# Slot beginnings between the last features, reciprocals spread by TensorE, output weights in the last slots, and RWKV factors without GpSimd

## The chip, the cores and the metric

The kernel runs on one core of one Trainium2 chip. The metric is the device time of one execution in microseconds, here as the median of a few runs. The engines of the core are named as the profile names them: PE is TensorE (matmuls; PEld its weight loads), DVE is VectorE, ACT is ScalarE, POOL is GpSimd, and SP is SyncE, which issues all DMAs of this kernel in one queue.

## What is computed

One inference step of a two-layer backbone for 1024 latent tokens and 128 prompt tokens, width 1024. Each layer projects the modulated input into three head groups, combines them in one output projection and adds it to the residual stream. The three parts that the change touches:

```python
def rwkv_step(S, inp):
    r_t, w_t, k_t, v_t, kk_t, a_t = inp
    sa = jnp.einsum('ebhvk,ebhk->ebhv', S, -kk_t)
    S = (S * w_t[..., None, :] + sa[..., :, None] * (kk_t * a_t)[..., None, :]
         + v_t[..., :, None] * k_t[..., None, :])
    return S, jnp.einsum('ebhvk,ebhk->ebhv', S, r_t)
...
    def one_block(args):
        qn_b, qr_b = args
        s = (jnp.einsum('bqhd,bkhd->bhqk', qn_b, kn)
             + jnp.einsum('bqhr,bkr->bhqk', qr_b, kr)).astype(jnp.float32) * SOFTMAX_SCALE
        p = jax.nn.softmax(s, axis=-1).astype(v.dtype)
        return jnp.einsum('bhqk,bkhd->bqhd', p, v)
...
    out = jnp.concatenate([y_rw, y_mla, y_lru], axis=-1) @ P['w_out'][l]
    x = layer_norm(ALPHA * x + gate * out, P['ln_g'][l], P['ln_b'][l])
```

The RWKV scan (4 heads, 2 directions) is done in chunks of 64 tokens: with cumulated decays every token's key, receptance and removal vectors become factors, and a chunk is a few small matmuls and a triangular inverse.

## The kernel before

Prompt and latent tokens stand in one array of 1152 columns, 9 tiles of 128 tokens, 18 chunks of 64. Operands of the large products are split in two parts (`mm3`: high x high, high x low, low x high). Each of the two layers goes through these stages.

*Token projections and queries*, then *features*: `order` lists 16 blocks of 128 columns of the input projection; for each, `feature(n_, j)` computes three blocks of 384 tokens, 24 matmuls each, into a PSUM tile `ps_a`, of which there are three. From the tenth feature on `RW_AT` starts `rwkv_tile(i)` for the 9 tiles: the **factor stage**. `rwkv_tile` loads the tile (`rw`), the key norms (`nkk`, in the single buffer `mxb`), computes log decays `lw_` and their cumulated sums `Lc` (two scans), and for each direction `d` the four factors: `z` and `r` in `abz` (`zr`), `k` and `b` in `ls` (`bk`), written to DRAM. Three of the products are made by GpSimd (lines 585, 593, 594). Between the features also stand pieces of the adaLN projection (`adaln_piece`), whose row `ep` is copied from PSUM by DVE before TensorE may use it.

*Beginnings*: nine value products `value(i)` and a tenth for the prompt, the prompt's two attention units (`ups`), and everything that the slot plan puts into slots -6 to -1: keys, loads and splits of queries, first row maxima (`max_q`, into the single PSUM tile `ps_b`), the first windows of the RWKV scan and their inverse. All of it stands in one block at a raised priority (line 1247), so a scheduler may put it ahead of work that was written before it.

*Slots*: 16 attention units (8 heads, two halves of 512 latent tokens) of three slots each, 48 slots a layer. A slot has fixed blocks A0, three score products, G, A1, B, values, C, sums, S; `at(slot, block, f, ...)` puts pieces of the RWKV windows, the adaLN rest, the next units' row maxima and group norms into them. In the slots the order of PE, DVE and ACT is the order of the code (`in_line`); DMAs and GpSimd are placed by the scheduler. At its last slot a unit's row sums are in PSUM; `sums` copies them, sends them through DRAM (`l_d`) to 128 x 4, `finish` takes the reciprocal there, sends it through DRAM again to 128 x 256 (`lr`), and `gate` multiplies.

*Output projection*: the 16 blocks of the output weights are loaded (`kp`), split into `wo_h` and `wo_l`, the gate rows are loaded and their bias added by GpSimd, the first weights of the next layer are loaded and split, and then nine output tiles follow, in `ORDER` (8, 2, 3, 4, 5, 6, 1, 0, 7), each 48 matmuls of 512 columns.

## Time and profile before

| what | value |
|---|---|
| median of three runs | 2005.73 us (2003.27 to 2010.9) |
| the profiled execution | 2003.78 us, span of its instructions 2001.9 us |
| busy share of the span | PE 91%, PEld 76%, DVE 60%, ACT 46%, POOL 34% |
| mean granted TensorE clock | 0.944 of full speed |
| layer 0: factors, beginnings, slots, hand-over | 336 to 448, to 512, to 889 (43 slots) and 940 us |
| layer 1: the same | 1340 to 1440, to 1491, to 1863 (43 slots) and 1890 us |

The granted clock of 1.00 is 2.4 GHz, half of it 1.2 GHz; a mean between them says for how much of a stretch the lower level held. A busy matmul side is not a matmul side at its peak. The rows below come from one profiled execution; windows are microseconds from the start of its span. In the rows DVE, ACT and PE stand with line 116 and 121, those of the helpers that record every instruction, so groups are told apart by their tiles.

### The profile page before, as it was taken

Reading aid. Unit: us, or ns where it says so; the run is one execution under the profiler, and the core shown is the slowest. Engines: PE = TensorE matmul, PEld = TensorE weight load, DVE = VectorE, ACT = ScalarE, POOL = GpSimd, SP = SyncE. Lnnn points to the kernel's source line nnn. Section 1 sums busy time; section 2 is a strip of 40 time slices with the busy share of each in tenths; the row PEclk is TensorE's granted clock in tenths of the full one; section 3 lists DMA queues with packets and bytes.
Section 4 is the critical chain, followed back from the end, with each engine's and each line's share of the span. In section 5 each row is a group of like instructions: output and inputs, shape, how many; then the busy total and the mean of one; then the engine's idle time right before and its main releaser. Section 6 shows DMA issues by size and latency. Waiting matters only on the chain.

```text
span 2001.9 us, 47694 instructions
## 1 busy us (share of the span) xinstructions
PE 1815.0 (91%) x18494; PEld 1527.9 (76%) x18494; DVE 1202.3 (60%) x2472; ACT 924.4 (46%) x2069; POOL 684.7 (34%) x1159
## 2 busy tenths in 40 slices
PE   6899998888899999994998999997779999998898
PEld 4798887786687787763877999997657778776686
DVE  6744445883456565764778443569735565666476
ACT  2533566442454554553235426675325455555421
POOL 1410011461434434322545100126424444441353
PEclk8999999887899999997998999998869999999999
DMA  8334444653335444437443252435533443334542
GB/s 298 109 96 153 131 122 139 208 179 107 90 95 126 115 114 103 118 107 221 151 138 111 93 173 87 121 113 173 172 84 66 108 93 99 89 89 141 154 155 85
DMA packets 346242, 256.34 MB, mean 128 GB/s; under 512 B 116968, under 2 KB 285600, under 8 KB 344992
## 3 DMA queue, kind: packets, MB, share of 16 engines
q1 hardware_dynamic: 346016, 253.30, 43.3%
q8 instruction: 145, 2.38, 0.5%
q14 instruction: 81, 0.66, 0.1%
HBM read 174.38 MB, written 78.78 MB: 126 GB/s over the span
## 4 chain that ended last, share of the span: by engine, by line
PE 68%; DVE 12%; DMA 10%; ACT 3%; issue 3%; SPq 2%; POOL 1%; DVEq 0%; ACTq 0%; POOLq 0%
PE ps_a L121 46%; PE ps_pv L121 7%; PE ps_b L121 5%; PE ps_rw L121 4%; PE ps_cx L121 4%; DVE ls L116 4%; DVE rw L116 3%; DVE sm L116 2%; DVE t L116 1%; DMA mxb<-inv_d 1%; DMA kp<-in_wout_dram 1%; DMA t<-zr_d 1%; DMA ls<-l_d 1%; DMA l_d<-sm 1%; ACT t L116 1%
## 5 line engine op out<-in xcount | busy, mean ns | idle before, releaser
L121 PE MATMUL ps_a<-t,t 128*128 128x384 f32 (+3 forms) x6048 | 708.8, 296 | 20.7 <-DVE t L116 5.4
L121 PEld LDWEIGHTS ps_a<-t,t 128*128 128x128 f32 (+1 forms) x6048 | 650.9, 167 | 48.5 <-ACT pe L116 14.1
L116 DVE TENSOR_REDUCE sm<-ps_b 128x1 f32<-128x1024 f32 (+1 forms) x164 | 181.3, 1106 | 123.4 <-PE ps_b L121 122.1
L121 PE MATMUL ps_a<-q,t 128*128 128x512 f32 (+1 forms) x912 | 233.6, 402 | 8.9 <-DVE ep L116 4.0
L116 ACT ACTIVATE pe<-ps_a 128x512 f32<-128x512 f32 (+1 forms) x296 | 168.3, 575 | 137.1 <-PE ps_a L121 125.3
L121 PEld LDWEIGHTS ps_a<-q,t 128*128 128x128 f32 x912 | 172.7, 198 | 54.1 <-issue 11.5
L121 PE MATMUL ps_a<-t,q 128*128 128x512 f32 (+1 forms) x544 | 161.6, 381 | 0.0
L116 DVE TENSOR_TENSOR t<-kp,t 128x512 fp32r<-128x512 f32 (+2 forms) x128 | 86.5, 704 | 87.9 <-ACT t L116 87.6
L121 PE MATMUL ps_a<-t,kp 128*128 128x512 f32 (+1 forms) x304 | 118.0, 390 | 22.7 <-DVE kp L116 22.7
L121 PE MATMUL ps_b<-t,q 96*128 96x512 f32 (+1 forms) x400 | 116.2, 388 | 22.9 <-DVE sm L116 17.0
L116 ACT CAST t<-kp 128x512 fp32r<-128x512 f32 (+2 forms) x128 | 73.3, 601 | 119.8 <-DMA kp<-in_wft_dram 47.7
L121 PE MATMUL ps_pv<-pe,t 128*64 128x256 f32 x928 | 125.3, 391 | 0.0
L121 PEld LDWEIGHTS ps_a<-t,q 128*128 128x128 f32 x544 | 100.0, 188 | 21.9
L520 POOL TENSOR_TENSOR rw<-rw 128x512 f32<-128x512 f32 (+1 forms) x24 | 20.0, 832 | 263.8 <-ACT rw L116 172.8
L121 PEld LDWEIGHTS ps_b<-t,q 96*128 96x128 f32 x400 | 67.5, 201 | 50.0 <-DVE sm L116 23.3
L855 POOL TENSOR_TENSOR t<-t 64x15 f32<-64x15 f32 (+2 forms) x270 | 72.4, 268 | 76.9 <-DVE t L116 43.0
L116 DVE TENSOR_TENSOR t<-ps_a,t 128x512 f32<-128x512 f32 (+2 forms) x106 | 65.5, 625 | 40.3 <-ACT t L116 33.5
L157 POOL TENSOR_TENSOR sm<-sm,nhalf 128x1 f32<-128x1 f32 (+1 forms) x54 | 34.3, 637 | 155.5 <-DVE sm L116 150.1
L121 PEld LDWEIGHTS ps_pv<-pe,t 128*64 128x64 f32 x928 | 59.8, 137 | 34.2 <-issue 8.6
L121 PEld LDWEIGHTS ps_a<-t,kp 128*128 128x128 f32 x304 | 58.3, 192 | 35.4 <-DVE kp L116 23.5
L1066 POOL TENSOR_TENSOR q<-q,q 96x512 fp32r<-96x512 f32 x36 | 47.3, 1314 | 100.6 <-ACT q L116 99.2
L121 PEld LDWEIGHTS ps_cx<-t,t 128*64 128x64 f32 (+1 forms) x1752 | 65.5, 138 | 20.3 <-ACT t L116 8.9
(258 smaller groups left out, 3253.7 us busy)
## 6 DMA issues: line engine op xcount, KB each, us to landing
kp<-in_wft_dram SPq DMA_DIRECT2D x64, 256.0 KB
kp<-in_wmod_dram SPq DMA_DIRECT2D x64, 256.0 KB
rw<-in_x_dram SPq DMA_DIRECT2D x36, 256.0 KB
gate_d<-pe SPq DMA_DIRECT2D x48, 192.0 KB
bk_d<-ls SPq DMA_DIRECT2D x36, 256.0 KB
zr_d<-abz SPq DMA_DIRECT2D x36, 256.0 KB
t<-bk_d SPq DMA_DIRECT2D x18, 512.0 KB
t<-zr_d SPq DMA_DIRECT2D x36, 256.0 KB
```

The lines of the kernel that those rows point to most:

```text
L116: return lambda *a, **k: in_line(getattr(self.eng, op)(*a, **k))
L121: return in_line(nc.tensor.matmul(*a, **k))
L157: gtt(out, t[:, :n], nhalf.to_broadcast([128, n]), op=POW)
L520: gtt(q_, a_, a_, op=MUL)
L855: gtt(tv, U_[0:64, 0:t, t:t + 1].to_broadcast([64, t, n]), X[0:64, t:t + 1, t:16].to_broadcast([64, t, n]), op=MUL)
L1066: gtt(qo[0:96], ql, qh[0:96], op=SUB)
```

## The change

`rwkv_tile`: the difference `Lc - lw_`, its exponential and GpSimd's three products go. The exponentials of `Lc` shifted by one token serve for `z`; the two products of each direction that are left are made by DVE, and the scale-and-add of `lw_` and of `k` and the copies into `wcs` by ScalarE. `finish`: the reciprocal is taken by DVE on the 128 x 128 sums in PSUM (`rl`), and four small matmuls with a constant (`two`) spread it over the output rows; no DRAM is passed; the factor 1/64 stands in the copy of the values (`u["o"]`). The gate's input is loaded earlier (`load_gate`), and GpSimd makes the last product. The beginnings are written out by hand between the parts of the last two features (`features` has become a generator), without the raised priority. The output weights are loaded and split in the last five slots, the gate rows get their bias in `adaln_piece`, the first output tiles are loaded before the last unit is finished, and the next layer's first weights come after two output tiles.

```diff
@@ rwkv_tile
-            vec_.tensor_scalar(fl(lw_), fl(tw), LWS, LWS, op0=MUL, op1=ADD)
+            act(fl(lw_), fl(tw), AF.Copy, bias=LWS, scale=LWS)
...
-                gtt(z, ch(Lc[:, d]), ch(lw_[:, d]), op=SUB)
-                act(z, z, AF.Exp)
                 act(r, ch(Lc[:, d]), AF.Exp)
                 act(b, ch(Lc[:, d]), AF.Exp, scale=-1.0)
                 if d == 0:
-                    vec_.tensor_copy(wcs[:, 0, q0:q0 + 2].rearrange("p q f -> p f q"), zr[:, :, :, 1, 63])
+                    sca_.copy(wcs[:, 0, q0:q0 + 2].rearrange("p q f -> p f q"), zr[:, :, :, 1, 63])
...
-                gtt(z, z, ch(nkk), op=MUL)
-                gtt(r, r, ch(r_), op=MUL)
+                at_, of_, end_ = (slice(1, 64), slice(0, 63), 0) if d == 0 else (slice(0, 63), slice(1, 64), 63)
+                sca_.copy(z[:, :, end_], ch(nkk)[:, :, end_])
+                vtt(z[:, :, at_], r[:, :, of_], ch(nkk)[:, :, at_], op=MUL)
+                vtt(r, r, ch(r_), op=MUL)
                 for f in range(2):
-                    vts(bk[:, f, :, 1], ta[:, d, f].rearrange("p (c t) -> p c t", c=2), kah[:, f:f + 1], omk[:, f:f + 1], op0=MUL, op1=ADD)
+                    act(bk[:, f, :, 1], ta[:, d, f].rearrange("p (c t) -> p c t", c=2), AF.Identity, bias=omk[:, f:f + 1], scale=kah[:, f:f + 1])
@@ sums, finish, gate
-                    ls = u["ls"] = W("ls", [128, 512])
-                    sca_.copy(ls[:, 0:128], u["sum"][:, 0:128])
-                    l_d = dram([4, 128], "l_d", 3)
-                    dma(l_d, ls[0:128:32, 0:128])
-                    u["lq"] = T("sm", [128, 16])
-                    dma(u["lq"][:, 0:4], l_d.rearrange("q (a c) -> (q a) c", c=4))
+                    u["rl"] = W("ls", [128, 128])
+                    vec_.reciprocal(u["rl"], u["sum"][:, 0:128])
...
+            ps = [P("a") for _ in range(2)]
+            for q_ in range(4):
+                r, c = (q_ // 2, q_ % 2) if u["q0"] < NS else (q_ % 2, q_ // 2)
+                R_ = slice(32 * q_, 32 * q_ + 32)
+                mm(ps[c][64 * r:64 * r + 64, 0:128], lhsT=two[R_], rhs=u["rl"][R_], start=True, stop=True)
+            for c in range(2):
+                vtt(u["o"][:, 128 * c:128 * c + 128], ps[c][:, 0:128], u["o"][:, 128 * c:128 * c + 128], op=MUL)
...
-            vtt(gm, gm, u["lr"], op=MUL)
+            gtt(gm, gm, u["o"], op=MUL)
@@ the plan of the slots
+        for x in range(2 * KT):
+            s_ = nslot - 5 + 5 * x // (2 * KT)
+            at(s_ - 1, "C", wo_load, x)
+            at(s_, "G", wo_split, x)
+        at(nslot - 1, "C", load_gates)
@@ the beginnings (cut)
+        more(2)
+        early(-6)
+        more(2)
+        early(-5)
...
+        early(-4)
+        value(0)
+        prompt_keys(0)
+        early(-3)
+        value(1)
+        max_last(ups[0])
+        value(2)
+        max_rows(ups[0])
+        early(-2)
...
@@ after the slots
+        load_out(0)
         finish(us[-1])
         gate(us[-1])
...
-        if l + 1 < layers:
-            w1 = first_weights(l + 1)
         for n_, i in enumerate(ORDER):
+            if n_ > 1:
+                load_out(n_)
+            if n_ == 2 and l + 1 < layers:
+                w1 = first_weights(l + 1)
```

How the change moves instructions is seen in three places. The first is VectorE in the factor stage of layer 0, one tile in its middle. `mxb` is the scaled key norm, `abz` holds z and r, `ls` holds k and b, `t<-kp` is a weight split and `pe` a gate feature. Before:

```order
L116 TENSOR_SCALAR ls_3589<-rw_617_3548,hv_278 128x2x64 x2
L116 SCALAR_TENSOR_TENSOR mxb_3539<-rw_613_3538,vec_111,mxb_3539 128x128 x2
L116 TENSOR_TENSOR ls_3572<-ls_3572 128x4x64
L116 TENSOR_TENSOR ls_3589<-ls_3589,rw_613_3538 128x4x64
L116 SCALAR_TENSOR_TENSOR rw_617_3548<-rw_617_3548,mxb_3539 128x256 x2
L116 TENSOR_TENSOR ls_3589<-ls_3589 128x4x64
L116 SCALAR_TENSOR_TENSOR ls_3572<-rw_617_3548,ls_3572 128x4x64
L116 SCALAR_TENSOR_TENSOR ls_3589<-rw_617_3548,ls_3589 128x4x64
```

VectorE at the same tile with the change:

```order
L116 SCALAR_TENSOR_TENSOR mxb_3541<-rw_613_3540,vec_111,mxb_3541 128x128 x2
L116 SCALAR_TENSOR_TENSOR rw_620_3569<-kc,rw_616_3549 128x256 x2
L116 TENSOR_TENSOR ls_3574<-ls_3574,rw_613_3540 128x4x64
L116 SCALAR_TENSOR_TENSOR rw_617_3550<-rw_617_3550,mxb_3541 128x256
L116 TENSOR_TENSOR t_4076<-kp_4089,t_4075 128x4x128
L116 TENSOR_TENSOR abz_3573<-abz_3573,mxb_3541 128x4x63
L116 TENSOR_TENSOR ls_3574<-ls_3574 128x4x64
L116 TENSOR_TENSOR ls_3590<-ls_3590,rw_613_3540 128x4x64
L116 SCALAR_TENSOR_TENSOR rw_617_3550<-rw_617_3550,mxb_3541 128x256
L116 SCALAR_TENSOR_TENSOR ls_3574<-rw_617_3550,ls_3574 128x4x64
L116 TENSOR_TENSOR abz_3589<-abz_3589,mxb_3541 128x4x63
```

The scale-and-add on `ls` has left VectorE's row, and the product of `abz` with the key norm, which GpSimd made, has come into it.

The second place is TensorE near the end of the features of layer 0. `ps_a<-t` are feature products, `kp,cS` and `kc,ep` an adaLN piece, `q,ckvh` value products, `ps_b` row maxima. Before, after the last feature:

```order
L121 MATMUL ps_a_4531<-kp_4527,cS 32x128 x4
L121 MATMUL ps_a_4531<-kp_4528,cS 32x128 x4
L121 MATMUL ps_a_4542<-kc,ep_4540 128x2
L121 MATMUL ps_a_4549<-q_4115,ckvh_326 128x512
L121 MATMUL ps_a_4549<-q_4116,ckvh_326 128x512
L121 MATMUL ps_a_4549<-q_4115,ckvl_327 128x512
L121 MATMUL ps_a_4554<-q_4115,ckvh_326 128x512
L121 MATMUL ps_a_4554<-q_4116,ckvh_326 128x512
```

TensorE with the change, three feature blocks before the last:

```order
L121 MATMUL ps_a_4436<-t_447,t_4076 128x384
L121 MATMUL ps_b_4612<-t_4113,q_4346 128x512 x2
L121 MATMUL ps_a_4469<-kp_4465,cS 32x128 x4
L121 MATMUL ps_a_4469<-kp_4466,cS 32x128 x4
L121 MATMUL ps_b_4640<-t_4113,q_4346 128x512 x2
L121 MATMUL ps_a_4480<-kc,ep_4478 128x2
L121 MATMUL ps_a_4483<-t_335,t_4075 128x384
```

The first row maxima, which stood behind the ten value products and the prompt, now stand among the features.

The third place is ScalarE in the last slots of layer 0. `pe` and `mxb` are exponentials of scores, `t<-kp` are splits of output weights, `ep` a unit's output. Before:

```order
L116 ACTIVATE pe_11068<-ps_a_11064 128x512
L116 CAST t_11146<-kp_11183 128x512
L116 CAST t_11146<-kp_11187 128x512
L116 CAST t_11146<-kp_11191 128x512
L116 COPY ep_11091<-ps_pv_10955 128x256
L116 CAST t_11146<-kp_11195 128x512
L116 COPY ls_11114<-ps_rw_10971 128x128
L116 CAST t_11147<-kp_11199 128x512
L116 CAST rw_1755_11258<-rw_1754_11256 128x512
```

ScalarE with the change, four slots before the last:

```order
L116 ACTIVATE pe_10867<-ps_a_10863 128x512
L116 ACTIVATE pe_10873<-ps_a_10869 128x512
L116 ACTIVATE mxb_10879<-ps_a_10875 128x512
L116 CAST t_10742<-kp_10840 128x512
L116 CAST t_10742<-kp_10842 128x512
L116 CAST t_10743<-kp_10844 128x512
L116 ACTIVATE ep_10921<-ps_pv_10727 128x256
L116 ACTIVATE pe_10947<-ps_a_10943 128x512
```

The splits that stood behind the last exponentials now stand between the exponentials of earlier slots.

## Rows read from the trace of the kernel before

**Rows 1.** Windows: start:end, length, busy us per engine (instructions), PE clock, DMA, GB/s.

```profile
336.00:448.00 112.00, 90.46 (x582) 84.53 (x581) 98.71 (x217) 54.59 (x160) 61.20 (x74) 0.88 0.56 184
448.00:512.00 64.00, 48.40 (x346) 37.99 (x346) 21.04 (x35) 15.88 (x39) 13.80 (x34) 0.72 0.41 119
512.00:889.00 377.00, 368.86 (x6158) 290.99 (x6157) 228.83 (x457) 192.72 (x433) 145.60 (x354) 1.00 0.43 107
889.00:940.00 51.00, 24.12 (x216) 14.50 (x214) 21.61 (x59) 21.67 (x45) 12.75 (x11) 0.77 0.67 205
1340.00:1440.00 100.00, 80.28 (x427) 74.19 (x426) 92.02 (x199) 47.91 (x148) 59.18 (x69) 0.86 0.46 156
1440.00:1491.00 51.00, 36.30 (x268) 26.90 (x268) 17.98 (x27) 13.78 (x35) 13.29 (x33) 0.67 0.49 135
1491.00:1863.00 372.00, 360.83 (x5891) 281.54 (x5890) 227.35 (x438) 196.62 (x443) 145.66 (x355) 0.99 0.39 97
1863.00:1890.40 27.40, 21.20 (x197) 13.27 (x197) 10.25 (x37) 13.28 (x30) 11.48 (x11) 0.98 0.49 144
```

**Rows 2.** Groups by form, 335 to 445: count | busy us, mean ns | idle before.

```profile
L116 DVE TENSOR_SCALAR ls<-rw,hv 128x128 f32<-128x128 f32 x35 | 16.8, 539 | 7.1 <-ACT rw L116 5.5 <-DMA bk_d<-ls 1.5
L116 DVE SCALAR_TENSOR_TENSOR rw<-rw,mxb 128x256 f32<-128x256 f32 x17 | 9.8, 603 | 0.0
L116 DVE SCALAR_TENSOR_TENSOR ls<-rw,ls 128x256 f32<-128x256 f32 x17 | 9.5, 578 | 0.1
L116 DVE TENSOR_TENSOR ls<-ls 128x256 f32<-128x256 f32 x17 | 9.2, 539 | 0.0
L116 DVE COPY wcs<-abz 128x4 f32<-128x4 f32 x18 | 7.1, 397 | 0.4 <-ACT abz L116 0.4
L116 DVE TENSOR_SCALAR rw<-rw 128x512 f32<-128x512 f32 x9 | 4.8, 539 | 0.2 <-ACT rw L116 0.2
...
L116 ACT ACTIVATE rw<-ps_rw,hv 128x128 f32<-128x128 f32 x36 | 10.5, 396 | 0.0
```

**Rows 3.** Timeline of layer 0's factors: start, us, engine, instruction.

```profile
343.60 0.84 POOL L594 TENSOR_TENSOR abz<-abz,rw 128x256 f32<-128x256 f32 x1 [0.24 <-DVE wcs L116]
343.77 0.96 DVE L116 TENSOR_TENSOR ls<-ls,rw 128x256 f32<-128x256 f32 x1
...
416.74 0.41 DVE L116 TENSOR_TENSOR ls<-ls,rw 128x256 f32<-128x256 f32 x1
```

**Rows 4.** Waits of PE, 336 to 448 and 448 to 512; chain of waits.

```profile
PE ps_a L121 <- DVE ep L116: 21.5, 5, 5.9
...
PE ps_b L121 <- DVE sm L116: 9.4, 6, 4.5
...
499.62 2.62 DMA ls<-l_d
```

**Rows 5.** Waits of PE from 889 to 941, and the chain of waits there.

```profile
PE ps_a L121 <- DVE kp L116: 21.5, 1, 21.5
...
929.98 7.07 DMA kp<-in_wtk_dram
```

**Rows 6.** Chain pieces in the slots of layer 0, and groups of VectorE by form.

```profile
862.06 1.45 PE ps_pv L121 x12
864.43 0.79 PE ps_rw L121 x24
...
L116 DVE RECIPROCAL sm<-sm 128x4 f32<-128x4 f32 x36 | 6.3, 174 | 20.6 <-DMA sm<-l_d 20.1
L116 DVE TENSOR_TENSOR_SCAN q<-rw,vec,q 128x512 f32<-128x512 f32 x8 | 10.3, 1283 | 0.2
L116 DVE TENSOR_REDUCE sm<-ps_b 128x1 f32<-128x1024 f32 x59 | 72.2, 1223 | 44.7 <-PE ps_b L121 43.9
```

**Rows 7.** Groups over the whole span: splits of weights on ScalarE and VectorE.

```profile
L116 ACT CAST t<-kp 128x512 fp32r<-128x512 f32 (+2 forms) x128 | 73.3, 601 | 119.8 <-DMA kp<-in_wft_dram 47.7 <-DMA kp<-in_wtk_dram 33.2 <-DMA kp<-in_wout_dram 28.3
L116 DVE TENSOR_TENSOR t<-kp,t 128x512 fp32r<-128x512 f32 (+2 forms) x128 | 86.5, 704 | 87.9 <-ACT t L116 87.6
```

More of the change, by code (lines that the diff above doesn't have):

```diff
@@ L689, in feature, with features @@
                 dma(gate_d[gi, :, bs], e)
-        for n_ in range(NFT):
-            if n_ == NFT - 2:
-                p_late = tc.cur_priority
+        def features(n_):
+            nonlocal ada_todo, wh, wl
             t = order[n_]
@@ L730, in hybrid_kernel @@
                 rwkv_tile(i)
+        for n_ in range(NFT - 2):
+            for _ in features(n_):
+                pass
         dma(lru_out[l], lru_fin)
@@ L746, in value @@
             (vec_.tensor_copy if i % 2 else sca_.copy)(val(i), ps)
-        for i in range(9):
-            value(i)
         lnx = sb.tile([128, 2, 2, 64], F32, name=f"lnx{l}", tag="lnx", bufs=1)
@@ L1123, in values @@
                     u["o"] = W("ep", [128, 256])
-                    sca_.copy(u["o"], u["pv"][:, 0:256])
+                    act(u["o"], u["pv"][:, 0:256], AF.Copy, scale=1 / 64)
         def sums(u):
@@ L1206, in hybrid_kernel @@
             at(s0 - 2, "S", max_rows, u)
-            if s0 + 5 < nslot:
-                at(s0 + 4, "G", finish, u)
-                at(s0 + 5, "G", gate, u)
-        for k_, todo_ in enumerate(ada_todo):
+            at(s0 + 2, "G", load_gate, u)
+            if s0 + 4 < nslot:
+                at(s0 + 3, "C", finish, u)
+                at(s0 + 4, "G", gate, u)
+        for k_, todo_ in enumerate(ada_todo[2:]):
             ada_ = adaln_piece(*todo_)
-            at(3 * k_ + 1, "S", next, ada_)
-            at(3 * k_ + 2, "A1", next, ada_, None)
-        ada_todo = []
+            at(5 * k_ // 2 + 1, "S", next, ada_)
+            at(5 * k_ // 2 + 2, "A1", next, ada_, None)
+        ada_todo = ada_todo[:2]
         CH = 7
@@ L1244, in hybrid_kernel @@
                     tail.append(gn)
-        with tc.high_priority(offset=tc.cur_priority - p_late):
-            value(9)
-            ups = [dict(h=4 * g, q0=NS, i=g, pe=[]) for g in range(2)]
-            for u in ups:
-                load_q(u)
-                split_q(u)
-            for g, u in enumerate(ups):
-                prompt_keys(g)
-                max_last(u)
-                max_rows(u)
-                scores(u, 0)
-                values(u)
-                sums(u)
-                finish(u)
-                gate(u)
-            for slot in range(min(s for s, _ in todo), 0):
-                for b in ("A0", "G", "A1", "B", "C", "S"):
-                    run(slot, b)
+        for x in range(2 * KT):
+            s_ = nslot - 5 + 5 * x // (2 * KT)
+            at(s_ - 1, "C", wo_load, x)
+            at(s_, "G", wo_split, x)
@@ new lines, in hybrid_kernel, with early, more, prompt @@
+        at(nslot - 1, "C", load_gates)
+        def early(slot):
+            for b in ("A0", "G", "A1", "B", "C", "S"):
+                run(slot, b)
+        assert min(s for s, _ in todo) == -6
+        last_features = (x for n_ in (NFT - 2, NFT - 1) for x in features(n_))
+        def more(n):
+            for _ in range(n):
+                next(last_features, None)
+        def prompt(u):
+            values(u)
+            sums(u)
+        ups = [dict(h=4 * g, q0=NS, i=g, pe=[]) for g in range(2)]
@@ new lines, in hybrid_kernel @@
+        for u, t_ in zip(ups, (promptq[:, 0:2], promptq[:, 2:4])):
+            u["qs"] = [t_[:, e] for e in range(2)]
+        more(2)
+        early(-6)
+        more(2)
+        early(-5)
+        more(1)
+        more(2)
+        for u in ups:
+            for t_ in u["qs"]:
+                nc.gpsimd.memset(t_[96:128].bitcast(F32), 0.0)
+            load_q(u)
+            split_q(u)
+            load_gate(u)
+        early(-4)
[3 more added lines that the diff above has]
+        value(1)
@@ new lines, in hybrid_kernel @@
+        max_last(ups[0])
+        value(2)
+        max_rows(ups[0])
+        early(-2)
+        value(9)
+        value(3)
+        scores(ups[0], 0)
+        prompt_keys(1)
+        value(4)
+        max_last(ups[1])
+        prompt(ups[0])
+        value(5)
+        early(-1)
+        max_rows(ups[1])
+        value(6)
+        scores(ups[1], 0)
+        value(7)
+        value(8)
+        finish(ups[0])
+        gate(ups[0])
+        prompt(ups[1])
+        todo.setdefault((0, "C"), []).insert(0, (finish, (ups[1],)))
@@ L1265, in hybrid_kernel @@
+        at(0, "S", gate, ups[1])
         line.update(on=True, last={})
@@ L1278, in hybrid_kernel, with load_out @@
         line["on"] = False
+        out_y = {}
+        def load_out(n_):
+            out_y[n_] = [W("pe" if n_ else "rw2", [128, 4, 128]) for _ in range(2)]
+            for j in range(2):
+                dma(out_y[n_][j], yT_d[ORDER[n_], :, 4 * j:4 * j + 4])
+        load_out(0)
         finish(us[-1])
```

75 lines of the change are left out of this document (37 added, 38 removed).

## The prediction

> **What bounds the kernel now.** First the page's engine shares, in the table above: TensorE's matmul side is busy 91% of the span, so a gain has to come from stretches where it is not busy or not at its upper clock. The stretches show where those are [rows 1]. The slots (512 to 889 and 1491 to 1863) have PE busy 368.86 of 377 and 360.83 of 372 us at a granted clock of 1.00 and 0.99, the upper level of 2.4 GHz: nothing to win there. Ahead of them in each layer lie two poorer stretches. While the RWKV factors are made (336 to 448, 1340 to 1440) PE is busy 90.46 of 112 us at clock 0.88 and 80.28 of 100 at 0.86, with DVE at 98.71 and 92.02 us: VectorE is the full engine, TensorE waits for it (21.5 us in five waits for the small `ep` copy alone, rows of which stand behind tile work in DVE's order [rows 4]) and falls to 1.2 GHz in between. Then come the beginnings of the slots (448 to 512, 1440 to 1491), where no engine is full, PE is busy 48.40 of 64 and 36.30 of 51 us and the clock is 0.72 and 0.67: a chain of single steps, one of them the reciprocals' trip through DRAM [rows 4]. After the slots of layer 0 (889 to 940) PE is busy 24.12 of 51 us; one wait of 21.5 us ends with DVE's split of the first output tile, which stood behind weight loads of the next layer [rows 5]. Layer 1 has less of that: 21.20 of 27.40 us.
>
> Counted at the upper clock, the work of TensorE is 90.46 x 0.88 + 48.40 x 0.72 = 114 us of the 176 from 336 to 512, and 80.28 x 0.86 + 36.30 x 0.67 = 93 of 151 in layer 1. So at most 62 + 58 us can be won ahead of the slots.
>
> **Factors without GpSimd.** A tile of 128 tokens is 2 directions; a layer has 9 tiles, 18 directions. DVE loses per layer 36 scale-and-add on 128 columns at 539 ns, 18 copies into `wcs` at 397 and 9 on 512 columns at 539: 19.4 + 7.1 + 4.9 = 31.4 us. It gains the two products that GpSimd did, 36 on 256 columns. While GpSimd works, such a DVE product takes 0.96 us, alone 0.41 [rows 3]; GpSimd's list is empty here afterwards, so I take 0.41: 14.8 us. The ends are 0.41 and 0.96 (34.6 us, which would eat the whole gain). The products that stay lose their slow share too: means of 603, 578 and 539 ns [rows 2] down to 415, 18 of each, 8.6 us. Net -25 us of DVE: 98.7 becomes 74 in layer 0, 92 becomes 67 in layer 1.
>
> ScalarE takes over: 36 on 128 columns at 396 ns (14.3 us), 9 on 512 columns at about the 601 of the weight casts [rows 7] (5.4), 36 tiny copies, not in the trace in this form; between 0.17 us, the smallest DVE row here [rows 6], and 0.40, I take 0.3 (10.8); it loses 18 exponentials, by the same row about 0.4 us each (7.2). Net +23: 54.6 becomes 78 and 47.9 becomes 71. So ScalarE is now fuller than VectorE. In the stage before, the fullest engine was busy 88% (98.71 of 112) and 92% (92.02 of 100). With ScalarE at the same shares: 78/0.88 = 88 us, **-24**, and 71/0.92 = 77 us, **-23**. TensorE's own 79.6 and 69.0 us fit in. GpSimd's missing work hides nothing: it was 61 us beside 112.
>
> **Beginnings woven in.** In the order of the change the keys and the first row maxima stand between the last feature products, and the ten value products, which stood in one row, are dealt out between the prompt's steps. Nothing is added but wait times get cover: each value product (3 matmuls) lies where a row maximum (1223 ns on DVE [rows 6]) or its way back through ScalarE is awaited. The trip through DRAM goes: `ls<-l_d` landed 2.62 us after issue, with a write, two more transfers and DVE's wait in front of it [rows 4]. What is late next is the chain row maximum, negation, scores of the first units, 9.4 us of PE's waits in this stretch [rows 4]; it starts earlier, under the features. The pure work is 34.8 and 24.3 us; with PE useful for 70% of the time (0.98 in the slots, 0.54 and 0.48 here before, so a middle) the stretches take 50 and 35 us: **-14** and **-16**. Ends: 0 if the chain stays as long, -26 each at the slots' own share.
>
> **Reciprocals by TensorE.** Per unit (16 a layer and 2 of the prompt) four matmuls of 32 rows, 64 output rows, 128 columns. The nearest row is the sums, 24 records for 12 matmuls of 128 columns in 0.79 us, four side by side [rows 6]: 4 x 0.066 = 0.26 us; if only two run side by side, as the value products (12 records, 6 matmuls of 256 columns, 1.45 us): 0.48. For 32 units in the slots 8.4 us (to 15), in a stage that TensorE bounds, so it counts in full. DVE's reciprocal now has 128 elements a partition, not 4. The trace has 4 elements at 174 ns, and as its slowest operation by element the scan, 512 in 1283 ns [rows 6]; by those 128 take between 0.3 and 0.5 us. It stands ahead of the next row maximum. The second row maximum of a slot can't start on TensorE before the first is reduced, since that PSUM tile has one buffer; between them lie the nine score matmuls, about 2 us, and the reduction is 1.2 us, so up to 0.8 us of reciprocal is covered. Gone from DVE: waits for `l_d`; gone from SP: five transfers a unit. I take **+7** for both layers together.
>
> The Trainium skill (VectorE: DVE Perf Modes, "First, the fixed hardware budget") says that the reciprocal is an iterative divide with a repeat count of 8. At the page's 0.96 GHz that would be an estimate of 1.1 us for 128 elements and some 1.2 with the fixed part; no row here has a long reciprocal to set against it. By the page the cover of 0.8 us would be overrun and the sum would be some 13 us higher, 1929.
>
> **Output weights in the last slots.** 16 splits (ScalarE 601 ns, DVE 704 [rows 7]) move into the last five slots. There layer 1 has ScalarE 13.3 and DVE 10.3 us of 27.4; with 9.6 and 11.3 more both are at 22 to 23 us, level with PE's 21.2. So five slots at about 27 us with some waiting for the loads (256 KB each; ScalarE waited 28.3 us for such loads in the trace [rows 7]), and 4 us for the last reciprocals and the split of the first tile (its load now precedes the last unit's finish): 31 us. Layer 0: 51 becomes 31, **-20**. Layer 1: 27.4 becomes 31, less some 4 us of earlier waits for those loads: **0**. The next layer's first weights move behind two output tiles, under matmuls. The gate's bias row costs a 2x128 addition in place of a copy: nothing.
>
> **Sum.** -24 - 23 - 14 - 16 + 7 - 20 + 0 = -90 against the profiled execution's 2003.8 us (span 2001.9 and 1.9 around it): 1914. The median of three runs is 2005.7, 2 us above; I forecast **1916**.
>
> **Rivals.** (a) *ScalarE becomes the bound.* Exponentials, copies and negations now share one in-order queue with the features' evacuations, on which TensorE's three `ps_a` buffers hang; for it speaks 78 us against DVE's 74, against it that it still has a third of its time free. Then the factor stages save 6 us each and the beginnings 10: -12 - 20 + 7 - 20 = -45: 1961. (b) *TensorE runs nearly full.* 114 and 93 us at 93% take 123 and 100: -53 - 51, with -24 at the end and +2: -126, 1880. For it speaks that all three engines have room, against it that in-order queues rarely mesh so well. (c) *The row maxima wait behind the reciprocals.* If a reciprocal is as slow as a row maximum (1223 ns [rows 6]), it overruns its cover by 0.4 us in each of 32 units: +13, 1929. Against it: the slowest row by element gives 0.5. The Trainium skill's price above is on the side of this case. (d) *The order changes but not the waits:* slot 0 still hangs on the inverse chain through GpSimd and two DRAM trips; the stages stay, the end saves 20: 1993. (e) *Slower.* The finish takes two of three `ps_a` buffers in the slot's middle and DVE frees them late; TensorE then idles in every unit and falls to the lower clock, as it does at 0.72 in the beginnings. It outweighs the gain of 97 us from 3.0 us a unit on; at 3.5 us (one wait and half a dip of clock), 32 units cost 112: 2021. Against it: DVE is busy 61% there (228.83 of 377).
>
> **How the numbers follow.** My forecast 0.54 (own range 1892 to 1938), (a) 0.17, (b) 0.13, (c) 0.08, (d) 0.04, (e) 0.04. The range 1875 to 1965 takes in (a), (b) and (c). A change within 0.5% (10 us) can't be told from none: (a), (b), (c) and the forecast are faster, 0.92; (d) 0.04 the same; (e) 0.04 slower.
>
> **What would show it.** Right: DVE products of 256 columns near 0.41 us throughout the factor stage, which takes 77 to 88 us; slot 0 some 38 us earlier in layer 0; clock at 2.4 GHz through most of the beginnings; the first output matmul within 5 us of the last slot. Wrong: `pe` or `abz` on ScalarE as what TensorE waits for (a); DVE's row maxima starting late behind a reciprocal over 0.8 us (c); TensorE waiting for `ep` in the slots (e).

## The result and the profile after

The changed kernel takes 1927.69 us (median of four runs, 1925.95 to 1929.34), the kernel before on the same chip 2004.86 us: a ratio of 0.961, 95% interval 0.9587 to 0.9633. The forecast was 1916 with a range of 1875 to 1965, so sign and range were right, and 77 of the 90 us came. The profiled execution has a span of 1927.3 us at a mean clock of 0.969 (before 0.944).

First the page's engine shares of the changed kernel (busy us, share of the span, instructions):

```profile
PE 1802.6 (94%) x18782; PEld 1510.9 (78%) x18782; DVE 1177.3 (61%) x2454; ACT 944.1 (49%) x2159; POOL 588.9 (31%) x1055
```

Then its stretches, to be set against [rows 1]: from the first factor tile to the last feature product and from there to slot 0, the slots and the hand-over, of both layers. Columns: start:end, length, busy us of PE, PEld, DVE, ACT and POOL (instructions), granted PE clock, DMA share, GB/s.

```profile
337.00:452.20 115.20, 101.93 (x643) 94.16 (x642) 79.29 (x195) 73.37 (x230) 19.20 (x23) 0.91 0.64 210
452.20:479.80 27.60, 25.12 (x292) 19.03 (x292) 15.75 (x26) 12.27 (x30) 10.88 (x35) 1.00 0.37 103
479.80:885.30 405.50, 397.49 (x6494) 306.37 (x6492) 252.70 (x522) 205.15 (x453) 151.32 (x359) 0.99 0.43 112
885.30:892.30 7.00, 2.37 (x15) 1.74 (x16) 4.32 (x9) 1.97 (x4) 0.00 (x0) 0.80 0.93 302
1280.60:1379.90 99.30, 92.20 (x551) 86.48 (x551) 71.98 (x179) 76.58 (x227) 16.50 (x20) 0.98 0.60 198
1379.90:1419.00 39.10, 30.48 (x276) 22.73 (x276) 25.38 (x42) 15.49 (x43) 17.87 (x47) 0.87 0.41 122
1419.00:1809.20 390.20, 384.67 (x6206) 294.51 (x6204) 243.92 (x488) 204.92 (x453) 149.78 (x355) 1.00 0.38 95
```

Factor stage and beginnings now run into each other, so the fair comparison is from the first factor tile to the first scores of slot 0. Cut at the starts of the same TensorE instructions in both traces, the stages are:

| stage | before, us | after, us | change | predicted |
|---|---|---|---|---|
| up to the first factor tile, layer 0 | 336.6 | 336.9 | +0.3 | 0 |
| first tile to slot 0, layer 0 | 174.9 | 142.8 | -32.1 | -38 |
| slots of layer 0 | 405.5 | 405.2 | -0.3 | +3.5 |
| last sums to first output product | 23.3 | 7.3 | -16.0 | -20 |
| output of layer 0, up to layer 1's first tile | 379.4 | 388.4 | +9.0 | 0 |
| first tile to slot 0, layer 1 | 171.4 | 138.3 | -33.1 | -39 |
| slots of layer 1 | 393.6 | 389.9 | -3.7 | +3.5 |
| last sums to first output product | 5.8 | 6.7 | +0.9 | 0 |
| the rest | 111.5 | 111.7 | +0.2 | 0 |

How far one trace can be trusted shows in a second trace of the changed kernel (the run `after_same` below): its stages to slot 0 take 140.5 and 134.8 us, its slots 404.8 and 390.2, its hand-overs 6.7 and 8.4, the output of layer 0 388.6. So between single traces a difference of some 3 us in a stage to slot 0, or of 2 at a hand-over, can't be told from none, while the slots repeat within 0.4 us.

The beginnings show what the weaving did: behind the last feature product TensorE is busy 25.12 of 27.60 us at the upper clock, where [rows 1] have 48.40 of 64 at 0.72. In the factor stage neither VectorE nor ScalarE is full: DVE 79.29 and ACT 73.37 of 115.20 us. What TensorE waits for there, in the row beside [rows 4] (engine and tile, waited for, us in total, times, longest), and then in the output (first row) and at the hand-over (second row) of layer 0:

```profile
PE ps_a L121 <- DVE ep L116: 9.0, 4, 3.6
```

```profile
PE ps_rw L124 <- DVE ls L116: 5.3, 1, 5.3
PE ps_a L121 <- DVE ls L116: 4.7, 1, 4.7
```

The prices, from the groups by form of the factor stage of layer 0 and of the whole span (instruction, shapes, count | busy us, mean ns | idle before):

```profile
L116 DVE TENSOR_TENSOR abz<-abz,mxb 128x252 f32<-128x252 f32 x18 | 7.4, 414 | 0.0
L116 DVE TENSOR_TENSOR ls<-ls,rw 128x256 f32<-128x256 f32 x18 | 7.5, 417 | 4.0 <-ACT ls L116 3.9
L116 DVE SCALAR_TENSOR_TENSOR rw<-rw,mxb 128x256 f32<-128x256 f32 x18 | 7.4, 418 | 0.0
L116 ACT ACTIVATE ls<-rw,hv 128x128 f32<-128x128 f32 x36 | 15.9, 495 | 0.5 <-DMA bk_d<-ls 0.5
L116 ACT COPY wcs<-abz 128x4 f32<-128x4 f32 x18 | 3.5, 194 | 0.1
L116 ACT COPY abz<-mxb 128x4 f32<-128x4 f32 x18 | 3.2, 197 | 6.4 <-DVE mxb L116 6.4
```

```profile
L116 DVE RECIPROCAL ls<-ps_rw 128x128 f32<-128x128 f32 x36 | 34.4, 956 | 9.5 <-PE ps_rw L121 9.1
```

The new products on VectorE take 414 and 417 ns, the price that was counted for them (0.41). The three of [rows 2] that stay, 603, 578 and 539 ns there, take 418, 475 and 436. On ScalarE the scale-and-add of k takes 495 ns, not the 396 that were counted, and the small copies 194 and 197, not 300. A reciprocal takes 956 ns, twice the upper end of the forecast. The spread is 0.38 us of TensorE's row in a slot, from one start to the next (start, duration, engine, instruction):

```profile
872.28 0.45 PE L121 MATMUL ps_a<-ls,two 32*64 32x128 f32 x8
872.65 0.63 PE L124 MATMUL ps_a<-kc,rw 128*64 128x128 f32 x4
```

### The profile page after: what moved, and what is told of

It is laid out like the page before. It is cut to its first block, busy times and chain, and to the rows that moved or that the text cites. A ratio compares the mean times of both kernels' runs of the same rounds, so it can differ in the third digit from the quotient of the medians.

```text
span 1927.3 us, 47961 instructions
## 1 busy us (share of the span) xinstructions
PE 1802.6 (94%) x18782; PEld 1510.9 (78%) x18782; DVE 1177.3 (61%) x2454; ACT 944.1 (49%) x2159; POOL 588.9 (31%) x1055
## 4 chain that ended last, share of the span: by engine, by line
PE 56%; DVE 7%; DMA 6%; ACT 4%; issue 3%; POOL 1%; SPq 1%; DVEq 0%; POOLq 0%; ACTq 0%
PE ps_a L121 36%; PE ps_pv L121 7%; PE ps_b L121 5%; PE ps_cx L121 4%; PE ps_rw L121 4%; DVE rw L116 2%; DVE sm L116 2%; DVE ls L116 1%; DVE t L116 1%; ACT rw L116 1%; ACT t L116 1%; DMA mxb<-inv_d 1%; ACT pe L116 1%; POOL rw L1416 1%; DMA kp<-in_wout_dram 1%
## 5 line engine op out<-in xcount | busy, mean ns | idle before, releaser
L121 PE MATMUL ps_a<-t,t 128*128 128x384 f32 (+4 forms) x6096 | 710.5, 295 | 20.7 <-DVE t L116 7.5
L121 PE MATMUL ps_a<-q,t 128*128 128x512 f32 x864 | 221.3, 401 | 4.9 <-DVE ep L116 4.9
L121 PEld LDWEIGHTS ps_a<-q,t 128*128 128x128 f32 x864 | 161.2, 190 | 47.9 <-issue 7.5
L121 PE MATMUL ps_b<-t,q 96*128 96x512 f32 (+1 forms) x384 | 107.3, 374 | 2.6 <-ACT t L116 1.5
L861 POOL TENSOR_TENSOR t<-t 64x15 f32<-64x15 f32 (+2 forms) x270 | 71.9, 266 | 58.9 <-DVE t L116 22.0
L116 ACT ACTIVATE rw<-rw,sm 128x512 f32<-128x512 f32 x35 | 26.7, 809 | 119.6 <-DVE sm L116 115.9
L121 PEld LDWEIGHTS ps_b<-t,q 96*128 96x128 f32 x384 | 61.9, 190 | 25.3 <-issue 9.9
L862 POOL TENSOR_TENSOR t<-t 64x15 f32<-64x15 f32 (+2 forms) x270 | 73.0, 270 | 20.4
L121 PE MATMUL ps_rw<-pe,two 128*32 128x128 f32 x1888 | 75.5, 277 | 0.0
```

Of the source, the lines that this page charges most:

```text
L116: return lambda *a, **k: in_line(getattr(self.eng, op)(*a, **k))
L121: return in_line(nc.tensor.matmul(*a, **k))
L861: gtt(tv, U_[0:64, 0:t, t:t + 1].to_broadcast([64, t, n]), X[0:64, t:t + 1, t:16].to_broadcast([64, t, n]), op=MUL)
L862: gtt(X[0:64, 0:t, t:16], X[0:64, 0:t, t:16], tv, op=ADD)
```

## The experiments

Each group of runs has runs of the kernel before beside it, on the same chip; kernels are compared by their ratios to it, where 0.001 is 2 us. The changed kernel has 0.961 (above) and 0.9621 (0.9597 to 0.9645) in the last group of runs.

**Factors made as before.** The body of `rwkv_tile` is the old one; all else is the changed kernel.

```diff
-            act(fl(lw_), fl(tw), AF.Copy, bias=LWS, scale=LWS)
+            vec_.tensor_scalar(fl(lw_), fl(tw), LWS, LWS, op0=MUL, op1=ADD)
...
+                gtt(z, ch(Lc[:, d]), ch(lw_[:, d]), op=SUB)
+                act(z, z, AF.Exp)
...
+                gtt(z, z, ch(nkk), op=MUL)
+                gtt(r, r, ch(r_), op=MUL)
```

> The changed kernel with the factors made as before: GpSimd's difference and three products, the exponential of z, the scale-and-add and the small copies on VectorE. If the prediction's sum holds (24 us in layer 0 and 23 in layer 1 belong to this part, whatever stands around it): 1928 + 47 = 1975 us. If the woven beginnings give TensorE other work while VectorE is late, so that part of the longer factor stage is covered: about half of it, 1950. If VectorE's longer row also makes the woven row maxima late, which now stand in the same queue: more than 47, about 1985. The stage from the first tile to slot 0 was 174.9 and 171.3 us before and is 142.8 and 138.4 now; it should read 166, 154 or 172 us in layer 0.

Measured: 0.9779 (0.9753 to 0.9805), so this part is worth some 33 us where it stands among the woven beginnings, not 47. The stage to slot 0 is 155.0 and 155.1 us, 12 and 17 longer. VectorE is busy 102.47 of 124 us, and the waits for `ep` are back, as in the kernel before (window of the stage up to 460 us, and waits of TensorE in the whole stage):

```profile
336.00:460.00 124.00, 99.83 (x619) 93.07 (x620) 102.47 (x219) 57.19 (x166) 66.02 (x80) 0.88 0.60 192
```

```profile
PE ps_a L121 <- DVE ep L116: 20.4, 5, 5.8
```

**The factors alone.** The kernel before with the new body of `rwkv_tile`, the same edit the other way round.

> The kernel before with only the new factor code (GpSimd's work in a tile to VectorE and ScalarE). By the prediction's terms (24 and 23 us): a ratio of 0.977 to the kernel before. By the run without the weaving, whose stages from the first tile to slot 0 were 9.6 and 17.4 us shorter than before: 27 us, 0.987. If ScalarE becomes the bound (the prediction's rival a): 12 us, 0.994. VectorE's 256-column products should read near 0.42 us in all of them.

Measured: 0.9899 (0.9884 to 0.9914), 20 us. VectorE and ScalarE have fallen and risen as predicted, yet the stage to slot 0 is only 4 and 12 us shorter. The windows of layer 0 tell why: TensorE does more in the first 112 us (97.69 us at clock 0.92; [rows 1] had 90.46 at 0.88), but the beginnings behind it still take 58.5 us at 0.67. Cut at the last feature product, the part in front of it is 8 and 16 us shorter than in the kernel before (111.3 and 92.2 us, not 119.6 and 108.5), and what follows is 4 and 5 us longer (59.4 and 67.4, not 55.3 and 62.8).

```profile
339.80:452.00 112.20, 97.69 (x642) 91.10 (x641) 76.25 (x191) 71.57 (x226) 12.67 (x16) 0.92 0.58 194
452.00:510.50 58.50, 38.20 (x280) 28.57 (x281) 19.54 (x31) 14.25 (x36) 14.59 (x37) 0.67 0.41 110
```

```profile
PE ps_a L121 <- DVE ep L116: 14.5, 5, 4.9
```

**The beginnings in one block.** The last two features as in the kernel before, then the value products in a row, then the prompt's units and slots -6 to -1 at the raised priority; reciprocals and factors of the changed kernel.

```diff
-        last_features = (x for n_ in (NFT - 2, NFT - 1) for x in features(n_))
-        more(2)
-        early(-6)
...
+        with tc.high_priority(offset=tc.cur_priority - p_late):
+            value(9)
...
+            for slot in range(min(s for s, _ in todo), 0):
+                for b in ("A0", "G", "A1", "B", "C", "S"):
+                    run(slot, b)
```

> The changed kernel with the beginnings in one block behind the features again, at the raised priority (reciprocals still by TensorE, factors still without GpSimd). By the prediction's sum (14 and 16 us): 1928 + 30 = 1958 us. If the trip through DRAM was what made the beginnings long, and not their order: about 1940. If the weaving also covers waits of the factor stage: above 1958, up to 1975. In the first case the stretch from the last feature product to slot 0 has a granted clock near 0.7 again.

Measured: 0.9834 (0.9798 to 0.987), so the weaving is worth some 44 us, above the 30 of the sum. The stage to slot 0 is 22.5 and 15.7 us longer, and the stretch ahead of slot 0 is back at clocks of 0.74 and 0.66, although no unit goes through DRAM:

```profile
449.00:503.40 54.40, 39.30 (x320) 28.51 (x319) 21.73 (x33) 14.93 (x35) 12.83 (x30) 0.74 0.42 113
1404.00:1458.20 54.20, 40.15 (x287) 28.47 (x288) 24.18 (x39) 15.03 (x36) 15.25 (x35) 0.66 0.44 130
```

So the order made the beginnings slow, not the trip.

**Reciprocals through DRAM again.** The copy, the five transfers and the 128 x 4 reciprocal of the kernel before, the finish one slot later; the gate's input is loaded in `finish` again, and GpSimd and VectorE change their products back.

```diff
-                    u["rl"] = W("ls", [128, 128])
-                    vec_.reciprocal(u["rl"], u["sum"][:, 0:128])
+                    sca_.copy(ls[:, 0:128], u["sum"][:, 0:128])
+                    dma(l_d, ls[0:128:32, 0:128])
+                    dma(u["lq"][:, 0:4], l_d.rearrange("q (a c) -> (q a) c", c=4))
```

> The changed kernel with the reciprocals through DRAM again (sums copied by ScalarE, 128 x 4 reciprocal, two more trips; the finish one slot later, the gate product on VectorE). The prediction counted the spread by TensorE as a cost of 7 us: by that 1921 us. The traces show the slots at the same length with and without it (405.8 and 405.5 us, 393.9 and 390.2): by that the slots stay, 1928 within 3. If the trip is on the path where nothing covers it (behind the last unit, and at the prompt's units): 5 us and more per layer on top, 1938 or above, seen as a wait ahead of the first output tile.

Measured: 0.9636 (0.9609 to 0.9662), which can't be told from the changed kernel. By the traces the slots are 2.8 and 2.9 us longer and the hand-overs 2.1 and 2.6 shorter; the stages to slot 0 (139.8 and 135.6 us) are as in the second trace of the changed kernel. Inside the slots most units start their successor 0.3 to 0.6 us earlier, the price of the spread and at most a little of the reciprocal, and one unit gains more (below). The last three slots lose 5.7 us again in each layer: in layer 0 VectorE stands 7.10 us, up to 881.30, waiting for the trip (`ls<-l_d`), and behind it TensorE waits ahead of the last slot's sums:

```profile
PE ps_a L124 <- DVE rw L116: 6.4, 1, 6.4
```

The spread and the trip cost about the same.

**Every reciprocal twice.**

```diff
                     vec_.reciprocal(u["rl"], u["sum"][:, 0:128])
+                    rl2 = W("ls", [128, 128])
+                    vec_.reciprocal(rl2, u["sum"][:, 0:128])
```

> The changed kernel with every reciprocal of 128 x 128 taken twice (the second into a tile that nobody reads); one took 956 ns. If the cover of 0.8 us that the prediction counted is all there is, the second one comes on top in each of 32 units: 31 us, a ratio of 0.977 to the kernel before where the changed kernel has 0.961. If VectorE's free time in the slots (busy 253 of 405 us) takes it: 0.961 within 0.003. The hand-overs get 1 us longer in either case, as TensorE waits for a reciprocal there.

Measured: 0.9736 (0.9711 to 0.976), 23 to 25 us; the profiled execution was the fastest of its four and shows 14.2 of them. In it the slots are 4.4 and 14.0 us longer, 7.7 and 10.3 without the one slot told of below, or 0.5 to 0.7 us a unit for a second reciprocal that adds 0.81 us (two in a row take 1.77; it also takes a tile of `ls`, which was not tried by itself); the hand-overs are 1.6 and 0.7 us longer, which two traces can't tell from none. So the first reciprocal is covered, with some 0.1 to 0.3 us to spare, and the second overruns the cover.

**Output weights after the slots.** `wo_load`, `wo_split`, the gate rows, the first weights and the loads of the first output tiles where the kernel before has them.

```diff
-            at(s_ - 1, "C", wo_load, x)
-            at(s_, "G", wo_split, x)
...
+        for k in range(KT):
+            for j in range(2):
+                raw = W("kp", [128, 512])
...
+        if l + 1 < layers:
+            w1 = first_weights(l + 1)
```

> The changed kernel with the output weights, the gate rows, and the next layer's first weights after the slots again, as before. By the prediction (20 us in layer 0, nothing in layer 1): 1948 us. By the two traces' ledger (hand-over of layer 0 16 us shorter, of layer 1 1 us longer, output of layer 0 7.6 us longer, and 8 us lost over layer 0's slots, all due to this part): it would be worth next to nothing, 1928 to 1932. The hand-over of layer 0 (last sums to first output product) should be near 23 us again and the output stage of layer 0 103 us in place of 110.

Measured: 0.9648 (0.9617 to 0.968), 5 to 8 us slower by the ratios, with intervals that overlap the changed kernel's. The hand-over of layer 0 is 12.2 us, not 23; its output stage is 379.1 us, as before, layer 1's hand-over is 3.8 us shorter, and the slots are 6.3 and 4.4 us longer. So by the traces this part brought 5 us at the hand-over of layer 0, where the table has 16, and 11 in the slots, and gave 9 back in the output stage and 4 at the hand-over of layer 1. That the output stage is longer by it stands on all traces here: 382.5 to 390.4 us in the ten with the moved weights, 377.1 to 379.4 in the four without. The scheduler puts the loads into the last slots in either version; in this one the first of them are issued at 810 us, 80 us ahead of the slots' end:

```profile
810.39 1.54 SPq L1352 DMA_DIRECT2D kp<-in_wout_dram  x3
```

The other 11 us of the old hand-over do not belong to one part. In the run with the trip and the moved weights (above) the hand-over is 5.2 us; it takes both, the trip and the weights behind the slots, to make it 23.0 to 23.3, as in the three kernels that have both.

**The scale-and-add of k on VectorE.**

```diff
-                    act(bk[:, f, :, 1], ta[:, d, f].rearrange("p (c t) -> p c t", c=2), AF.Identity, bias=omk[:, f:f + 1], scale=kah[:, f:f + 1])
+                    vts(bk[:, f, :, 1], ta[:, d, f].rearrange("p (c t) -> p c t", c=2), kah[:, f:f + 1], omk[:, f:f + 1], op0=MUL, op1=ADD)
```

> The changed kernel with the 36 scale-and-add of k's factors per layer back on VectorE (on ScalarE they take 495 ns, 15.9 us in layer 0). If ScalarE is what bounds the stage, as the prediction's sum had it (78 us of work against 74): it gets faster, by up to 16 us a layer, ratio down to 0.945. If VectorE's order is what TensorE waits for (the waits for the small ep copy, 9.0 us in layer 0): slower, some 10 us a layer at 0.28 us each and the longer waits, 0.966 to 0.971. If neither engine bounds it: 0.961 within 0.003.

Measured: 0.9613 (0.9586 to 0.964): no difference over the whole. With ScalarE relieved the stage to slot 0 gets no shorter (it is 3.7 and 3.3 us longer in the trace, 6.0 and 6.8 against the second one), so ScalarE is not the bound. Layer 0's slots are 4 us shorter at the one slot below, which hides part of that in the total.

**The `ep` waits, in the changed kernel and in the one before.** In both, the second half of an adaLN piece (the small product that reads `ep`) goes two feature blocks later.

```diff
-            for todo in ada_todo[:ka]:
-                for _ in adaln_piece(*todo):
-                    pass
+            ada_pend.extend(adaln_piece(*todo) for todo in ada_todo[:ka])
+            for g_ in ada_pend:
+                next(g_)
...
+                if j == 1:
+                    ada_flush()
```

> The changed kernel with the second half of each adaLN piece between the features (the small product that reads the ep copy) put two feature blocks later. TensorE waited 9.0 us for that copy in layer 0's factor stage and 3 us ahead of it. If these waits are on the path: 9 to 13 us faster, a ratio of 0.955 to 0.9565 to the kernel before. If VectorE's row is late as a whole and the next wait takes their place: 0.961. The wait of TensorE for ep should be gone from layer 0 in both cases; the stage to slot 0 of layer 0 should read 131 to 134 us in the first.

Measured on the changed kernel: 0.9548 (0.9533 to 0.9564), 12 to 15 us faster. In the trace 6.8 us of it lie ahead of the first factor tile, where the waits for `ep` fall from 6.4 to 1.9 us, 4.0 us from there to slot 0 of layer 0 (1.7 against the second trace of the changed kernel; 138.8 us, not the 131 to 134 that were expected), and 3.1 us in layer 0's slots, by the one slot told of below. The wait for `ep` (9.0 us) is gone from the factor stage; in its place stand a wait for a load, and 1.5 us more for the gates' `pe`:

```profile
PE ps_a L121 <- DVE pe L116: 4.0, 2, 2.0
PE ps_cx L121 <- DMA ep<-hid_d: 3.0, 3, 1.4
```

> The kernel before with one edit alone: the second half of each adaLN piece between the features two feature blocks later. In its factor stage of layer 0 TensorE waited 21.5 us for the ep copy, with VectorE busy 98.71 of 112 us. If the full VectorE was the bound (the prediction's reading), other waits for it take that place: within 5 us of the kernel before, ratio 0.997 or above. If the place of the copy in VectorE's queue was the bound, and not its load: 15 to 21 us faster, 0.99 or below.

Measured on the kernel before: 1.0009 (0.9992 to 1.0025), nothing over the whole. It too reaches the first factor tile earlier, after 330.8 us and not 336.6; so do all four traces with the edit (327.3 to 330.8 us, where the ten others have 335.1 to 339.8). But the stages from there to slot 0 are 4.5 and 8.3 us longer (179.4 and 179.7 us): up to the last feature product nothing is won (120.7 us after 119.6 in layer 0), and the beginnings behind it are 3.4 and 5.5 us longer, for a reason that the runs don't show. In the factor stage the 21.5 us for `ep` turn into

```profile
PE ps_a L121 <- DVE pe L116: 16.0, 6, 4.8
```

So in the factor stage of the kernel before, with VectorE busy 98.53 of 113 us in this run too, another of VectorE's results took the place of `ep`, and nothing was won: there its load was the bound. In the changed kernel the waits that took the place of `ep` (4.0 and 3.0 us) are smaller, and the stage got no longer. About half of the 12 to 15 us, though, come from ahead of the factor stage, where the edit saves as much in either kernel.

**Two more edits on top, and the changed kernel beside them.** First the output weights one slot earlier, then in addition the first weights behind the seventh output tile's norms.

```diff
-            s_ = nslot - 5 + 5 * x // (2 * KT)
+            s_ = nslot - 6 + 5 * x // (2 * KT)
```

```diff
-            if n_ == 2 and l + 1 < layers:
-                w1 = first_weights(l + 1)
...
+            if n_ == 7 and l + 1 < layers:
+                w1 = first_weights(l + 1)
```

> The changed kernel itself, as the base of the runs beside it: a ratio of 0.961 within 0.002 to the kernel before.

> The changed kernel with the second halves of the adaLN pieces later (which alone gave a ratio of 0.955) and the output weights one slot earlier, so that the last unit's reciprocal doesn't stand behind splits that wait for a load on VectorE. TensorE waited 4.7 and 4.1 us for that reciprocal at the two hand-overs. If the splits were what held it: some 6 us less, 0.952. If the loads only compete with the slots' own transfers one slot earlier: 0.955.

> The run beside it and, in addition, the next layer's first weights behind the seventh output tile's norms and not behind the second tile. In the changed kernel TensorE waited 5.3 us in the middle of layer 0's output for VectorE, which the weight splits had made late, and ran at half clock for 3 us after it; the stretch from the first output product to the next layer's factors went from 379.4 to 388.4 us. If the splits are the cause: 379 us again, some 8 us less than the run beside it, 0.948. If the later loads then make the next layer's first products wait: the same as the run beside it or slower.

Measured: 0.9621 (0.9597 to 0.9645), 0.9572 (0.9549 to 0.9594) and 0.9569 (0.9543 to 0.9596). Neither adds to what the `ep` edit gives by itself. At the first hand-over the wait for the reciprocal falls from 4.7 to 1.4 us, but TensorE then waits for the `ep` product; the hand-over is 6.7 us, no shorter. In the output stage with the late first weights the wait for `ls` is 1.2 us, not 5.3 (6.1 in the second trace of the changed kernel). But with the `ep` edit alone, and the first weights where they were, it is small already:

```profile
PE ps_rw L124 <- DVE ls L116: 1.8, 1, 1.8
```

The stretch is 386.5 us, not 379 (386.3 with the `ep` edit alone, 383.9 in the run beside it): with the late first weights the output stage and the next layer's first products have these waits

```profile
PE ps_a L121 <- POOL t L341: 4.5, 2, 4.0
PE ps_a L121 <- DVE t L116: 2.9, 1, 2.9
PE ps_rw L124 <- DVE ls L116: 1.2, 1, 1.2
```

So a later place for the first weights does not shorten the stretch. That the moved weights and tile loads as a whole make it longer is shown by the run that put them back (379.1 us); which of these edits does stays open. The lowest ratio is that of the changed kernel with the `ep` edit, 0.9548; the two versions with more can't be told from it.

## Why the prediction came out right, and where its steps did not

**What bounds the kernel** held. VectorE filled the factor stage (moving the `ep` product alone won nothing in it), the beginnings were slow by their order and ran at a granted clock of 0.72 and 0.67, and the slots gave next to nothing.

**Factors, -47: the mechanism right, the size too big.** The prices came out or nearly (new products 0.41 us; VectorE 79.29 us over a somewhat longer stretch where 74 was forecast, ScalarE 73.37 where 78 was). The step that failed is the last one, "with ScalarE at the same shares: 78/0.88 = 88 us". That rule takes for granted that an engine below its old load bounds the stage in the same way. It does not: ScalarE can be relieved by 16 us a layer, at VectorE's cost, with no gain, and TensorE was left with its own work and a wait for `ep` (9.0 us). And the gain of this part counts only as far as what follows can start earlier: 20 us alone, where the block of beginnings stays, 33 us among the woven ones.

**Beginnings, -30: right, too small.** Taken out they cost some 44 us. The step that was mis-sized is "PE useful for 70% of the time (0.98 in the slots, 0.54 and 0.48 here before, so a middle)". Behind the last feature it is 25.12 of 27.60 us at the upper clock, 91%, in layer 0, and 30.48 x 0.87 of 39.10, 68%, in layer 1; and a part of the beginnings lies inside the factor stage, in time that was waited there. (The upper end of 26 us that the forecast gives "each" is 28 in layer 0: 64 less 34.8/0.98.) Factors and beginnings together were forecast at 77 and measured at 65.

**Reciprocals, +7: no cost that shows.** TensorE's price was inside the bounds (0.38 us a unit; 0.26 to 0.48), but the trip that it replaces was taken to cost nothing in the slots, and its last three slots cost 5.7 us in each layer (above). VectorE's price was not inside: 956 ns against "between 0.3 and 0.5 us", since the rows that set those ends were other operations. The scan is not the slowest by element there either: [rows 2] have 539 ns for 128 columns. The Trainium skill's rule (VectorE: DVE Perf Modes, "First, the fixed hardware budget"), by which the estimate was 1.1 us, was much the nearer. But what rival (c) made of a slow reciprocal did not follow: the slots are 0.3 and 3.7 us shorter, not longer, and only a second reciprocal shows in the time. The cover is larger than the 0.8 us that were counted from the score products alone. So the price was too low and the cover too short, and the two errors cancel: that is luck.

What was not foreseen is one slot of each layer, the thirteenth. From the starts of the score products it takes 9.8 or 9.9 us in all four kernels with the DRAM trip and 10.3 to 15.9 in the ten traces with the spread. The rows of the changed kernel (start, duration, engine, instruction, idle before) show the queue:

```profile
579.16 0.29 DVE L116 COPY t<-t 32x256 f32<-32x256 f32 x1 [2.61 <-DMA t<-N_d]
579.47 0.96 DVE L116 RECIPROCAL ls<-ps_rw 128x128 f32<-128x128 f32 x1
...
580.35 0.23 DVE L116 COPY ep<-ps_a 128x128 f32<-128x128 f32 x1
580.49 1.21 DVE L116 TENSOR_REDUCE sm<-ps_b 128x1 f32<-128x1024 f32 x1
...
580.63 0.97 PE L121 MATMUL ps_a<-q,t 128*128 128x512 f32 x3 [1.87 <-DVE ep L116]
```

A copy on VectorE waits 2.61 us for a load, the reciprocal stands behind it, the copy that frees a `ps_a` tile behind that, and TensorE's scores wait 1.87 us for that tile. The slot pays more than this wait, since its granted clock is 0.89, between stretches at 1.00:

```profile
577.00:592.00 15.00, 12.98 (x152) 9.64 (x151) 7.69 (x15) 4.39 (x9) 8.69 (x31) 0.89 0.43 122
```

The load decides, and not the reciprocal's length. In the ten traces with the spread, the slot takes 10.3 or 10.4 us with one reciprocal (11.0 with two) where the copy starts before the slot's first scores, and 11.8 to 15.9 where it starts 1.1 to 2.3 us after them. With the trip the copy starts in time in all eight of these slots. Why the load is late only with the spread, and not in every version, is not shown. By its sign, a wait for `ep`, this is rival (e) in one unit of sixteen, but the tile is held by the adaLN row's copy, not by the finish. A wait for a load in front of the reciprocal makes the hand-over too:

```profile
886.79 0.62 ACT L116 CAST t<-kp 128x512 fp32r<-128x512 f32 x1 [2.08 <-DMA kp<-in_wout_dram]
887.44 0.69 DVE L116 TENSOR_TENSOR t<-kp,t 128x512 fp32r<-128x512 f32 x1 [1.39 <-ACT t L116]
888.92 0.96 DVE L116 RECIPROCAL ls<-ps_rw 128x128 f32<-128x128 f32 x1
889.93 0.70 PE L121 MATMUL ps_a<-ls,two 32*64 32x128 f32 x8 [4.67 <-DVE ls L116]
```

**Hand-over, -20 and 0.** It measured -16 and +0.9. The -16 can't be put down to the moved weights alone: without them the hand-over is 12.2 us with the spread, and with them 5.2 us with the trip. The sentence that failed is "The next layer's first weights move behind two output tiles, under matmuls": TensorE was covered, but VectorE was not. It waited for the splits' other half ahead of the first tile's own product:

```profile
901.95 0.69 DVE L116 TENSOR_TENSOR t<-kp,t 128x512 fp32r<-128x512 f32 x1 [4.61 <-ACT t L116]
902.56 0.68 DVE L116 TENSOR_TENSOR rw<-ps_a,t 128x512 f32<-128x512 f32 x1
```

It stayed late: in the kernel before, its product of the tile waited for TensorE (988 to 1018 us), where it now waits for nothing (0.0 us from 940 to 970, in the row at the end):

```profile
L116 DVE TENSOR_TENSOR rw<-ps_a,t 128x512 f32<-128x512 f32 x5 | 3.4, 685 | 2.8 <-PE ps_a L121 2.8
```

TensorE met it at the next layer's first transposes with a wait of 5.3 us. The output of layer 0 became 9.0 us longer, a term that the sum did not have at all. That these splits make it is only argued: moving them did not give the 9 us back, and with the `ep` edit the stretch stays at 383.9 to 386.5 us although this wait is 1.8 us or less.

Between the two traces the sum came out 15 us too low: 12 in the two stages to slot 0, 9 in the output, 5 at the hand-overs, less 11 in the slots. That the total came this near is partly luck, since these errors have both signs.

**The rivals.** (a) is refuted by the scale-and-add on VectorE. (b) was not reached, 127.05 us busy at 0.93 in 142.8 being 83% and not 93. (c) was right that the reciprocal is long and wrong about what follows from it. (d) is excluded by the result; the sign of (e) shows in one unit of a layer. Of the signs named for the forecast, slot 0 came 32 us earlier in layer 0 (38 forecast), and the first output product 7 us after the last sums, not within 5.

## What to carry to other kernels

When the fullest engine of a stage is relieved, do not scale the stage with the next one's load: look for the one small result that another engine waits for in order, and move its reader. Over the whole kernel that brought nothing before the change and 12 to 15 us after it, about half of them ahead of the stage. A long operation put into an in-order queue costs little by its length and much by its place: look for a wait on a load in front of it (the slot of 10.3 us that becomes 14.3) and for whoever waits behind it. And a gain ahead of a chain counts only as far as the chain can move up with it.

## What the runs showed of the hardware

A reciprocal of 128 elements a partition takes 956 ns on VectorE, where a product with two operands of 256 takes 417. In the output stage of layer 0 (940 to 970 us), while GpSimd works, VectorE's additions of two operands of 512 in SBUF take 1780 ns; over the whole execution the seven that lie beside a GpSimd operation take 1.77 us and the eight that meet none 0.68. The products with one operand in PSUM take 675 ns there, in GpSimd's pauses. But over the whole execution the eleven of them beside a GpSimd operation take 0.69 us and the 17 that meet none 0.68, so these are not slowed:

```profile
L116 DVE TENSOR_TENSOR rw<-rw,t 128x512 f32<-128x512 f32 x6 | 10.7, 1780 | 5.0 <-POOL rw L1416 5.0
L116 DVE TENSOR_TENSOR rw<-ps_a,t 128x512 f32<-128x512 f32 x5 | 3.4, 675 | 0.0
```
